# Twenty-one streams of unread matmuls, with other orders of the moving columns, between the memory stage and layer 0 of an encoder

## The chip, the core and the metric

The kernel runs on one core of a Trainium2 chip. The core has five engines that run side by side and meet through semaphores: TensorE (matmuls, PE in the profile, its weight loads PEld), VectorE (DVE), ScalarE (ACT), GpSimd (POOL) and SyncE (SP, which here issues the transfers). SBUF is the on-chip memory of 128 partitions that the engines read, PSUM the one that matmuls write. The metric is the time of one execution on the device in microseconds (us).

## The reference

A trunk of two layers over 256 tokens of width 2048 in float32. Each layer projects the normed tokens with one wide matrix, runs a short gated convolution, a differential attention and a cross-attention into 256 memory tokens on parts of the result, and projects back:

```python
for l in range(DEPTH):
    h = rmsnorm(x, norm_g[l])
    proj = h @ w_in[l]
    ...
    mn = rmsnorm(mem, mem_norm_g[l])
    mkv = mn @ w_mem_kv[l]
    ...
    y = jnp.concatenate([y_a, y_d, y_m], axis=-1) @ w_out[l]
    x = x + y
```

w_in[l] is 2048 x 7168, w_mem_kv[l] 2048 x 1024 and w_out[l] 2048 x 2048, so nearly all the work is in these products.

## The kernel before

Every large product is done in three matmuls of type float32r: each operand is split into a rounded part (hi) and the rest (lo), and the products hi*hi, hi*lo and lo*hi are summed in PSUM (L227, L228, L229). The stationary side is the transposed activation: memT for the memory, xT for a layer's input, yT for its mixed output. Each of these is one tile of 128 partitions x 2 parts x 16 slices x 256 tokens: part 0 is hi, part 1 is lo, and slice k holds the features 128k to 128k+127. So the hi part of a partition is one row of 4096 neighbouring float32r numbers, and slice k is its columns 256k to 256k+255. The moving side is the weight: block() (L218) computes 512 output columns for both halves of the tokens (NT = 2), and for each of the 16 slices of the weight there are 2 x 3 matmuls, so 96 in a block. A weight slice comes by DMA into raw (four buffers of two slices, issued by SyncE), ScalarE casts it to hi (L210, or L213 with a gain) and VectorE subtracts to get lo (L211, L214). hi and lo have eight buffers each, so eight slices can be in store ahead of TensorE.

The memory stage comes first: for each layer two blocks with memT (keys and values). During its later blocks, small pieces of other work run between the matmuls from a list called side. One of them, x_rows, transposes x on TensorE into the PSUM tile pt (L468), and split_T writes it into xT (ScalarE L192, VectorE L193). Behind the memory stage flush_side() ends the list, and the layers begin. Block 0 of layer 0 gives the first 512 columns of the attention's queries and keys; normed() computes their squares (ScalarE, L275), a sum and an inverse root in small steps on VectorE (L276 to L282) and the scaled result nat (L284). During block 1, qk_T transposes nat on TensorE into ptq (L356) and copies it into yT (ScalarE L364, VectorE L365).

The order in which each engine runs is not the order of the code. The program is built with a scheduler that simulates the engines and gives each of them its own list, in which independent pieces of code are interleaved. PSUM tiles come from pools: acc from ps_acc (four buffers), and the attention scores s from ps_s (two buffers). A tile that takes a buffer waits on a semaphore until the last users of that buffer are done.

Of the kernel before, what the change touches and what calls it, by code (L numbers as in the profile page):

```python
# [10 lines left out]
F32 = mybir.dt.float32  # L11
# [7 lines left out]
P = 128  # L19
# [13 lines left out]
NB = 512  # L33
# [10 lines left out]
def encoder(ctx: ExitStack, tc: tile.TileContext, x, mem, norm_g, w_in, conv_w, conv_b,  # L44
            dq_g, dk_g, lq1, lk1, lq2, lk2, head_g, mem_norm_g, w_mem_kv, mq_g, mk_g, w_out, out):
    nc = tc.nc
    x, mem, out = x[0], mem[0], out[0]

    def pool(name, bufs, space=None):
        kw = {"space": space} if space is not None else {}  # L50
        return ctx.enter_context(tc.tile_pool(name=name, bufs=bufs, **kw))
# [8 lines left out]
    ps_s = pool("ps_s", 2, PSUM)  # L60
# [121 lines left out]
    def flush_side():  # L182
        while side:
            run_side()
# [292 lines left out]
    def stats_of(parts, tag):  # L477
        ss = small.tile([P, NT], F32, tag="ssum", name=nm("ssum"))
        nc.vector.tensor_reduce(ss, parts, AX.X, ALU.add)
        return row_stats(ss, tag)  # L480

    def T_tile(what):
        return big.tile([P, 2, KT, SEQ], F32R, tag="T", name=nm(what))
# [38 lines left out]
    for l in range(DEPTH):  # L522
# [13 lines left out]
        if l == 0:  # L536
            side.append(turn(nat, [(mkT[l], 0, MH, cvb[:, 56 + l:57 + l])]))
            xT = T_tile("xT")
# [3 lines left out]
                    x_square(c, t)  # L542
    flush_side()

    for l in range(DEPTH):
        st = stats_of(ssx, "st")

# [105 lines left out]
        if l + 1 < DEPTH:  # L653
            xT = T_tile("xT")
        order = list(range(CG, KT)) + list(range(CG))
        for b in range(4):
            final = l + 1 == DEPTH
            acc = block(yT, w_out[l], [(b * NB, NB)], order, apart=4 if final and b == 3 else 0)
            for t in range(NT):
                n = 256 if final else NB  # L660
# [41 lines left out]
```

## Time and profile before

| | us |
|---|---|
| median of 2 runs (964.81 to 964.99) | 964.9 |
| the profiled execution's own time | 965.74 |
| its span, first to last instruction | 964.0 |

The profile is of one execution. In its groups of instructions a row has the line, the engine, the operation, output and inputs by their names in the program, the shapes and the count; then the busy time in all in us, the mean of one in ns, and the idle time of the engine in front of them. In its timeline a row has the start in us from the beginning of the span, the duration in us, engine, line and operation. In a table by stretches each row has the stretch, its length, then busy time and count of instructions of TensorE, its weight loads, VectorE, ScalarE and GpSimd, the clock granted to TensorE (1.00 is full), the share of the DMA engines that is busy and GB/s. The end of a matmul is modelled, since matmuls overlap: starts are what the pace is read from. The weight loads of float32r matmuls stand in the profile as rows of their own, and in the lists of instructions below they belong to the matmul.

### The profile page before, as it was taken

What the parts mean: (1) busy time and instruction counts of PE and PEld (TensorE: products, weight loads), DVE (VectorE), ACT (ScalarE), POOL (GpSimd) and SP (SyncE); (2) the same over time, 40 slices, a digit from 0 to 9 for tenths busy, and PEclk for the clock granted to TensorE, in tenths of its full rate; (3) what the DMA queues carried; (4) which work ended last, traced back from release to release, by engine and by line L of the source; (5) the groups of instructions that cost most, each with busy time, mean ns of one, the idle gap of its engine ahead of it and who ended that gap; (6) DMA issues with size and microseconds to landing.
All of it is one profiled execution on the core that took longest, in us unless ns stands there. A gap on an engine that the chain in (4) does not pass through costs nothing.

```text
span 964.0 us, 13420 instructions
## 1 busy us (share of the span) xinstructions
PE 956.4 (99%) x4485; PEld 791.5 (82%) x4485; DVE 671.1 (70%) x1496; ACT 561.1 (58%) x1103; POOL 1.4 (0%) x8
## 2 busy tenths in 40 slices
PE   9999999999999999999999999999999999999998
PEld 6788888888888888888888888888888888888886
DVE  5768568865787876567766678866787776578553
ACT  7676555765656655554555556754666655554442
POOL 0000000000000000000000000000000000000000
PEclk9999999999999999999999999999999999999999
DMA  8855666566555555555555666666555565555662
GB/s 293 281 182 182 185 189 187 175 198 195 175 169 160 156 172 162 168 174 175 189 182 178 194 176 181 180 207 197 153 172 177 155 176 154 175 174 175 217 217 68
DMA packets 101353, 175.26 MB, mean 182 GB/s; under 512 B 6190, under 2 KB 25764, under 8 KB 101284
## 3 DMA queue, kind: packets, MB, share of 16 engines
q1 hardware_dynamic: 100132, 173.36, 59.3%
q10 hardware_dynamic: 1152, 1.05, 0.3%
q8 instruction: 35, 0.57, 0.2%
q14 instruction: 34, 0.28, 0.1%
HBM read 172.29 MB, written 2.10 MB: 181 GB/s over the span
## 4 chain that ended last, share of the span: by engine, by line
PE 96%; ACT 1%; DMA 1%; DVE 0%; SPq 0%; issue 0%; DVEq 0%; ACTq 0%
PE acc L229 30%; PE acc L227 30%; PE acc L228 30%; PE po L330 2%; DMA raw<-in_w_mem_kv_dram 1%; PE ptT L323 1%; PE pt L468 1%; PE s L438 1%; PE s L392 1%; PE s L391 1%; ACT hi L213 1%; PE ptq L356 1%; ACT sq L519 1%; PE py L315 0%; PE pt L296 0%; PE pt L602 0%
## 5 line engine op out<-in xcount | busy, mean ns | idle before, releaser
L210 ACT CAST hi<-raw 128x512 fp32r<-128x512 f32 x576 | 356.3, 622 | 324.9 <-PE acc L229 200.0
L211 DVE TENSOR_TENSOR lo<-raw,hi 128x512 fp32r<-128x512 f32 x576 | 395.7, 690 | 209.8 <-ACT hi L210 204.9
L227 PE MATMUL acc<-hi,xT 128*128 128x512 f32 x896 | 354.0, 395 | 0.0
L228 PE MATMUL acc<-lo,xT 128*128 128x512 f32 x896 | 352.0, 393 | 0.0
L229 PE MATMUL acc<-hi,xT 128*128 128x512 f32 x896 | 351.7, 392 | 0.0
L227 PEld LDWEIGHTS acc<-hi,xT 128*128 128x128 f32 x896 | 168.4, 188 | 33.8
L229 PEld LDWEIGHTS acc<-hi,xT 128*128 128x128 f32 x896 | 168.4, 188 | 33.8
L228 PEld LDWEIGHTS acc<-lo,xT 128*128 128x128 f32 x896 | 168.5, 188 | 33.3
L228 PE MATMUL acc<-lo,yT 128*128 128x512 f32 x256 | 99.9, 391 | 0.0
L229 PE MATMUL acc<-hi,yT 128*128 128x512 f32 x256 | 99.2, 390 | 0.0
L227 PE MATMUL acc<-hi,yT 128*128 128x512 f32 x256 | 98.3, 392 | 0.0
L214 DVE SCALAR_TENSOR_TENSOR lo<-raw,cva,hi 128x512 fp32r<-128x512 f32 x64 | 47.3, 749 | 19.2 <-ACT hi L213 18.2
L213 ACT ACTIVATE hi<-raw,cva 128x512 fp32r<-128x512 f32 x64 | 44.9, 721 | 24.1 <-PE acc L229 12.1
L229 PEld LDWEIGHTS acc<-hi,yT 128*128 128x128 f32 x256 | 48.1, 188 | 10.0
L228 PEld LDWEIGHTS acc<-lo,yT 128*128 128x128 f32 x256 | 48.1, 188 | 9.7
L227 PEld LDWEIGHTS acc<-hi,yT 128*128 128x128 f32 x256 | 48.1, 188 | 9.7
L227 PE MATMUL acc<-hi,memT 128*128 128x512 f32 x128 | 51.9, 409 | 1.4 <-ACT memT L189 0.9
L228 PE MATMUL acc<-lo,memT 128*128 128x512 f32 x128 | 50.3, 394 | 0.0
L229 PE MATMUL acc<-hi,memT 128*128 128x512 f32 x128 | 48.5, 396 | 0.0
L227 PEld LDWEIGHTS acc<-hi,memT 128*128 128x128 f32 x128 | 24.3, 190 | 7.2 <-ACT memT L189 1.6
L228 PEld LDWEIGHTS acc<-lo,memT 128*128 128x128 f32 x128 | 24.4, 190 | 4.7
L229 PEld LDWEIGHTS acc<-hi,memT 128*128 128x128 f32 x128 | 23.9, 188 | 5.1 <-DVE memT L190 0.2
(150 smaller groups left out, 685.0 us busy)
## 6 DMA issues: line engine op xcount, KB each, us to landing
raw<-in_w_in_dram SPq DMA_DIRECT2D x192, 512.0 KB, 3.9
raw<-in_w_out_dram SPq DMA_DIRECT2D x64, 512.0 KB, 3.7
raw<-in_w_in_dram SPq DMA_DIRECT2D x64, 256.0 KB, 3.5
raw<-in_w_mem_kv_dram SPq DMA_DIRECT2D x31, 512.0 KB, 4.7
xs<-in_x_dram SPq DMA_DIRECT2D x4, 512.0 KB
xs<-in_mem_dram SPq DMA_DIRECT2D x3, 512.0 KB, 9.7
out_dram<-xs SPq DMA_DIRECT2D x8, 128.0 KB, 3.3
out_dram<-xs ACTq DMA_DIRECT2D x8, 128.0 KB
```

Source lines behind the costliest of these rows:

```text
L210: nc.scalar.copy(hi, raw[:, j])
L211: nc.vector.tensor_tensor(lo_, raw[:, j], hi.bitcast(F32), ALU.subtract)
L213: nc.scalar.activation(hi, raw[:, j], AF.Copy, scale=gains_of(j))
L214: nc.vector.scalar_tensor_tensor(lo_, raw[:, j], gains_of(j), hi.bitcast(F32), ALU.mult, ALU.subtract)
L227: nc.tensor.matmul(acc[t], sh, hi, start=first, stop=False)
L228: nc.tensor.matmul(acc[t], sh, lo, start=False, stop=False)
L229: nc.tensor.matmul(acc[t], sl, hi, start=False, stop=last)
L323: nc.tensor.transpose(pt[:, k, i * P:(i + 1) * P], e[:, i, k * P:(k + 1) * P], ident)
L330: nc.tensor.matmul(po[:, i, :], eT[:, k, i * P:(i + 1) * P], v[:, k, h * P:(h + 1) * P], start=k == 0, stop=k == NT - 1)
L356: nc.tensor.transpose(pt[:, j, :], nat[t][:, j * P:(j + 1) * P], ident)
L391: nc.tensor.matmul(s[c][:, i, :], qi, k_first(yT, c, h), start=True, stop=False)
L392: nc.tensor.matmul(s[c][:, i, :], qi, k_second(yT, k2, c, h), start=False, stop=True)
```

## The change

One function and 21 calls are added behind the flush_side() of the memory stage. Nothing else is touched.

```diff
@@ -542,6 +542,41 @@
                     x_square(c, t)
     flush_side()
 
+
+    flat = xT[:, 0].rearrange("p k t -> p (k t)")
+
+    def stream(name, base=512, run=None, jump=None, turned=False, n=6):
+        ps = ps_s.tile([P, NB], F32, tag="s", name=name)
+        o, mov = ps, flat[:, base:base + NB]
+        if run is not None:
+            mov = mov.rearrange("p (l q i) -> p q l i", i=run, q=jump // run)
+            if turned:
+                o = o.rearrange("p (l q i) -> p q l i", i=run, q=jump // run)
+        for j in range(n):
+            nc.tensor.matmul(o, flat[:, 0:P], mov, start=True, stop=True)
+
+    stream("prA")
+    stream("prB", run=2, jump=4)
+    stream("prC", run=2, jump=8)
+    stream("prD", run=2, jump=16)
+    stream("prE", run=2, jump=32)
+    stream("prF", run=2, jump=64)
+    stream("prG", run=2, jump=128)
+    stream("prH", run=2, jump=256)
+    stream("prI", run=4, jump=16)
+    stream("prJ", run=4, jump=64)
+    stream("prK", run=8, jump=16)
+    stream("prL", run=8, jump=64)
+    stream("prM", run=16, jump=32)
+    stream("prN", run=16, jump=256)
+    stream("prO", base=514)
+    stream("prP", base=516)
+    stream("prQ", base=520)
+    stream("prR", base=528)
+    stream("prS", run=2, jump=16, turned=True)
+    stream("prT", run=2, jump=64, turned=True)
+    stream("prU", base=514, run=2, jump=16)
+
     for l in range(DEPTH):
```

Each stream is six equal matmuls: the first 128 columns of xT's hi part are the stationary tile, 512 columns from base are the moving ones, and the product goes into a PSUM tile of the scores' pool, which nothing reads. With run and jump the same 512 columns are taken in another order: run neighbours, then the run that lies jump columns further on, and so on to the end of the 512, and then the same from the next run. prA to prR and prU write their output in the order in which the columns come. prS and prT are turned: they write each column to its own place, so the output jumps as the input does.

The scheduler does not put all of them in front of layer 0. TensorE's list at the end of the memory stage, before (xT_669 is xT; acc_1197 and acc_1198 are the two halves of block 0, with one number for each tile):

```order
L468 MATMUL pt_1093<-ident,xs 128x128 [waits DVE_49,PE_49]
L468 MATMUL pt_1093<-ident,xs 128x128 x3
L227 MATMUL acc_1197<-hi_1201,xT_669 128x512
L228 MATMUL acc_1197<-lo_1202,xT_669 128x512
L229 MATMUL acc_1197<-hi_1201,xT_669 128x512
```

And with the change, where acc_1344 and acc_1345 are the two halves of block 0:

```order
L468 MATMUL pt_1093<-ident,xs 128x128 [waits DVE_49,PE_49]
L468 MATMUL pt_1093<-ident,xs 128x128 x3
L556 MATMUL prA<-xT_669 128x512 x6
L556 MATMUL prB<-xT_669 128x512 x6
L227 MATMUL acc_1344<-hi_1348,xT_669 128x512
...
L227 MATMUL acc_1344<-hi_1370,xT_669 128x512
L556 MATMUL prC<-xT_669 128x512 [waits PE_49]
L556 MATMUL prC<-xT_669 128x512 x5
L556 MATMUL prD<-xT_669 128x512 [waits PE_49]
L556 MATMUL prD<-xT_669 128x512 x5
L228 MATMUL acc_1344<-lo_1371,xT_669 128x512
```

Two streams stand in front of block 0. The others follow two at a time, with 13 matmuls of the blocks between pairs: prC to prP in block 0, prQ to prT in block 1, and prU by itself behind them. From prC on the first matmul of each stream waits on TensorE's own semaphore, for the last users of its PSUM buffer.

The second place is in block 1, where TensorE transposes the queries and keys of block 0 (ptq_1427 and ptq_1458; acc_1403 and acc_1404 are the halves of block 1). Before:

```order
L227 MATMUL acc_1404<-hi_1517,xT_669 128x512
L228 MATMUL acc_1404<-lo_1518,xT_669 128x512
L356 MATMUL ptq_1427<-ident,nat_1398 128x128 [waits DVE_49,PE_49]
L356 MATMUL ptq_1427<-ident,nat_1398 128x128 x3
L356 MATMUL ptq_1458<-ident,nat_1401 128x128 [waits DVE_49,PE_49]
L356 MATMUL ptq_1458<-ident,nat_1401 128x128 x3
L229 MATMUL acc_1404<-hi_1517,xT_669 128x512
```

With the change (ptq_1574 and ptq_1605; acc_1550 and acc_1551 are the halves of block 1):

```order
L556 MATMUL prS<-xT_669 128x8x32x2 [waits PE_49]
L556 MATMUL prS<-xT_669 128x8x32x2 x5
L556 MATMUL prT<-xT_669 128x32x8x2 [waits PE_49]
L556 MATMUL prT<-xT_669 128x32x8x2 x5
L227 MATMUL acc_1551<-hi_1589,xT_669 128x512
...
L227 MATMUL acc_1550<-hi_1616,xT_669 128x512
L356 MATMUL ptq_1574<-ident,nat_1545 128x128 [waits DVE_49]
L356 MATMUL ptq_1574<-ident,nat_1545 128x128 x3
L356 MATMUL ptq_1605<-ident,nat_1548 128x128 [waits DVE_49]
L356 MATMUL ptq_1605<-ident,nat_1548 128x128 x3
L228 MATMUL acc_1550<-lo_1617,xT_669 128x512
L556 MATMUL prU<-xT_669 128x512 [waits PE_49]
```

In block 1 the transposes stood behind 59 of its matmuls. Now they stand behind 25 of them and the 24 of prQ to prT.

The third place is VectorE's list in block 1, the small steps between the squares of block 0 and nat. Before (lo_1518, lo_1536 are casts of block 1's slices 10 and 11):

```order
L159 TENSOR_SCALAR rsy_1384<-rsy_1384 128x16 [waits DVE_49]
L161 SCALAR_TENSOR_TENSOR rsa_1385<-rsy_1384 128x16 [waits DVE_49]
L211 TENSOR_TENSOR lo_1518<-raw_1511,hi_1517 128x512 [waits Activation_49]
L162 TENSOR_TENSOR rsa_1385<-rsa_1385,ss_1375 128x16 [waits DVE_49]
L163 SCALAR_TENSOR_TENSOR rsy_1384<-rsa_1385,rsy_1384 128x16 [waits DVE_49]
L161 SCALAR_TENSOR_TENSOR rsa_1385<-rsy_1384 128x16 [waits DVE_49]
L211 TENSOR_TENSOR lo_1536<-raw_1533,hi_1535 128x512 [waits DMAHW6_49,Activation_49]
```

With the change (lo_1665 is the cast of slice 10):

```order
L159 TENSOR_SCALAR rsy_1531<-rsy_1531 128x16 [waits DVE_49]
L161 SCALAR_TENSOR_TENSOR rsa_1532<-rsy_1531 128x16 [waits DVE_49]
L162 TENSOR_TENSOR rsa_1532<-rsa_1532,ss_1522 128x16 [waits DVE_49]
L163 SCALAR_TENSOR_TENSOR rsy_1531<-rsa_1532,rsy_1531 128x16 [waits DVE_49]
...
L284 TENSOR_TENSOR nat_1545<-acc_1344,rsy_1531 128x512 [waits DVE_49]
L284 TENSOR_TENSOR nat_1548<-acc_1345,rsy_1531 128x512 [waits DVE_49]
L211 TENSOR_TENSOR lo_1665<-raw_1658,hi_1664 128x512 [waits Activation_49]
```

The casts of slices 10 to 13 stood between the small steps. Three of them now stand behind nat, and the one of slice 13 behind the four copies of ptq into yT (L365). ScalarE's list changes in the same place and in the same way: its four copies of ptq (L364) now stand together, and so do its last two into xT (L192), with VectorE's last two (L193). The lists of SyncE and GpSimd are as before.

## The prediction

> **What bounds the kernel now.** I read the page first, then the waits of TensorE, then the stretches, and last the timeline at single instructions. The page's first rows and the chain of work that ended last:
>
> ```profile
> span 964.0 us, 13420 instructions
> PE 956.4 (99%) x4485; PEld 791.5 (82%) x4485; DVE 671.1 (70%) x1496; ACT 561.1 (58%) x1103; POOL 1.4 (0%) x8
> PEclk9999999999999999999999999999999999999999
> PE 96%; ACT 1%; DMA 1%; DVE 0%; SPq 0%; issue 0%; DVEq 0%; ACTq 0%
> ...
> L227 PE MATMUL acc<-hi,xT 128*128 128x512 f32 x896 | 354.0, 395 | 0.0
> L227 PEld LDWEIGHTS acc<-hi,xT 128*128 128x128 f32 x896 | 168.4, 188 | 33.8
> ```
>
> TensorE is busy for 956.4 of 964.0 us at full granted clock, and 96% of the chain is matmuls. A busy TensorE is not yet a TensorE at its pace, so the next question is whether it waits near the change. All waits of TensorE (time in total, times, longest), and stretches from the start, around the change and at the end:
>
> ```profile
> PE warm L112 <- DVE zeros L107: 1.2, 1, 1.2
> PE pt L468 <- DMA xs<-in_mem_dram: 1.1, 2, 0.9
> PE acc L227 <- ACT memT L189: 0.9, 1, 0.9
> PE acc L227 <- ACT hi L213: 0.5, 1, 0.5
> ...
> 0.00:20.00 20.00, 17.68 (x71) 11.76 (x72) 10.94 (x25) 16.08 (x37) 1.37 (x8) 1.00 0.84 291
> 20.00:50.00 30.00, 28.57 (x130) 22.62 (x129) 23.36 (x66) 18.45 (x33) 0.00 (x0) 1.00 0.83 282
> ...
> 100.00:120.00 20.00, 20.00 (x96) 16.55 (x94) 10.91 (x18) 12.55 (x22) 0.00 (x0) 1.00 0.60 171
> 120.00:150.00 30.00, 30.00 (x138) 24.94 (x137) 22.05 (x45) 16.37 (x28) 0.00 (x0) 1.00 0.62 186
> ...
> 900.00:964.00 64.00, 60.16 (x266) 49.48 (x264) 31.35 (x54) 23.03 (x37) 0.00 (x0) 0.99 0.51 165
> ```
>
> The second column is TensorE's busy time in each stretch. It stands idle for 2.3 us before 20 us, 1.4 us before 50 us, and 3.8 us at the end where only output is left. In the two stretches around the change it has no idle time at all. So there is no hole there which added matmuls could fill, and every matmul put in front of layer 0 pushes the end out by its own pace.
>
> **The pace of one matmul** is not its duration (395 ns in the group of the page), since the next one starts before the last one has drained. It is the distance between starts. Timeline of TensorE, start, duration, engine, line (PEld is the weight load):
>
> ```profile
> 94.31 0.39 PE L229 MATMUL acc<-hi,memT 128*128 128x512 f32 x1
> 94.31 0.19 PEld L227 LDWEIGHTS acc<-hi,memT 128*128 128x128 f32 x1
> 94.54 0.39 PE L227 MATMUL acc<-hi,memT 128*128 128x512 f32 x1
> 94.54 0.19 PEld L228 LDWEIGHTS acc<-lo,memT 128*128 128x128 f32 x1
> 94.76 0.39 PE L228 MATMUL acc<-lo,memT 128*128 128x512 f32 x1
> ...
> 196.35 0.39 PE L227 MATMUL acc<-hi,xT 128*128 128x512 f32 x1
> 203.83 0.39 PE L227 MATMUL acc<-hi,xT 128*128 128x512 f32 x1
> ```
>
> The last two rows are 33 matmuls apart: 7.48 / 33 = 0.2267 us each. The weight load of the next one (0.19 us) runs under it. In that stretch every sixth matmul waits on a semaphore of ScalarE and a weight tile changes each time, and both are inside the 0.2267.
>
> **The change, part by part.** It removes nothing. It adds 21 streams of 6 matmuls, 126 in all, each with a 128x128 stationary tile from xT, 512 moving columns from xT and a PSUM tile that nobody reads. They have the form of the rows above. No engine but TensorE gets an instruction, and no DMA is added.
>
> 1. 126 x 0.2267 = 28.6 us, if every order of columns streams at the pace of a contiguous one. The bound from below is the weight load, which each matmul has: 126 x 0.188 (mean of the LDWEIGHTS group above) = 23.7 us. No row of before reads its moving columns in another order than one run after the other, so the trace has no price for this. The bound from above is the slowest row per column, the plain fp32 scores of the memory heads:
>
> ```profile
> L438 PE MATMUL s<-mkT,mqT 128*128 128x256 f32 x32 | 8.2, 378 | 0.0
> ...
> 403.12 1.03 PE L438 MATMUL s<-mkT,mqT 128*128 128x256 f32 x4
> 403.80 0.58 PE L227 MATMUL acc<-hi,xT 128*128 128x512 f32 x1
> 404.22 0.39 PE L228 MATMUL acc<-lo,xT 128*128 128x512 f32 x1
> ```
>
> From 403.12 to 404.22 are four of them and one L227: (1.10 - 0.2267) / 4 = 0.218 us for 256 columns, so 0.437 us for 512. An order that halves the rate costs 0.437 - 0.227 = 0.21 us more per matmul, and if all 126 ran so the streams would take 55.1 us. I take the contiguous pace for all: five streams (A, O, P, Q, R) are contiguous in all but their start, and the other sixteen still read whole runs of 2 to 16 neighbours, so they are nearer to the rows at 0.2267 than to a form that runs at half rate because of its type. [...]
>
> 2. The seams. The streams stand in ten pairs and one single between the matmuls of blocks 0 and 1, so there are 22 seams. What a seam can cost is seen where TensorE changes its kind of work:
>
> ```profile
> 107.49 0.60 PE L468 MATMUL pt<-ident,xs 128*128 128x128 f32 x4
> 107.84 0.48 PE L227 MATMUL acc<-hi,xT 128*128 128x512 f32 x1
> 108.16 0.40 PE L228 MATMUL acc<-lo,xT 128*128 128x512 f32 x1
> ```
>
> The first L227 after transposes takes 0.32 us to the next start, 0.09 more than usual: at most 22 x 0.09 = 2.0 us. I take 0, because the streams have the type and shape of their neighbours and a change of tile alone costs nothing in the rows at 196 us. Nineteen streams (all but prA and prB) also wait for TensorE's own earlier matmuls, the last users of their PSUM buffer. Those are at least 11 matmuls back, so 11 x 0.2267 = 2.5 us, long past the 0.39 us that one takes. Queued behind such a wait is only TensorE's own order. 0.
>
> 3. The moved work. The eight transposes into ptq stood 59 matmuls behind the start of block 1 and now stand 49 behind it, 24 of them streams, so at 11.1 us instead of 13.4. They wait for VectorE's nat. VectorE now runs that chain of small steps with fewer casts (lo) between. Its rows in before, where block 1 starts at 129.74:
>
> ```profile
> 129.74 0.39 PE L227 MATMUL acc<-hi,xT 128*128 128x512 f32 x1
> 129.89 1.36 DVE L276 TENSOR_REDUCE ss<-sq 128x8 f32<-128x512 f32 x2
> 132.64 0.17 DVE L158 TENSOR_SCALAR rsy<-ss 128x16 int32<-128x16 int32 x1
> 132.84 0.17 DVE L159 TENSOR_SCALAR rsy<-rsy 128x16 int32<-128x16 int32 x1
> 137.05 0.36 DVE L282 TENSOR_SCALAR rsy<-rsy,st 128x8 f32<-128x8 f32 x2
> 138.00 1.28 DVE L284 TENSOR_TENSOR nat<-acc,rsy 128x512 f32<-128x512 f32 x2
> ```
>
> Up to L158 the order is as before (2.9 us behind the start of the block). Then 11 small steps of 0.2 us, 0.36 and 1.28 follow without casts: nat is there 6.8 us behind the start, 4.3 us ahead of the transposes that wait for it. The casts that VectorE puts off are those of the slices 10 to 13 of block 1. TensorE wants slice 10 behind 54 block and 30 stream matmuls and the transposes, 19.9 us in, and VectorE has it by 6.8 + 0.69 = 7.5 us. The four yT steps then hold VectorE until about 15 us, and slice 13 is wanted at 24.0. So nothing waits: 0. The cover is the eight slices of hi and lo in store, about 48 x 0.2267 = 10.9 us; were it gone, a late nat would hold TensorE for what it is late, and no more than these few us once.
>
> 4. SyncE's weight DMAs are neither moved nor added to. They come later with the buffers they wait for. ScalarE and VectorE get 28.6 us more for the same work. Since TensorE does not wait for them after 50 us, that wins nothing.
>
> Sum against the profiled execution: 964.0 + 28.6 = 992.6 us of span, 965.74 + 28.6 = 994.3 us for its own time. The median of the runs is 0.84 us under the profiled one: 964.9 + 28.6 = **993.5 us**. The likeliest case's own range is 992.0 to 995.5, the upper end with the 2.0 us of seams.
>
> **The rivals.**
>
> - Turned output. prS and prT also write PSUM in the pairs' order. If that alone runs at half rate, 12 x 0.21 = 2.5 us more: 996.0 us, and 1001 at a third or so of the rate. No row of before writes a matmul's output in short runs, and all of its outputs are contiguous, which speaks neither way. [...] Chance 0.12.
> - Pairs read at half rate. Eight streams read runs of 2 without turning (B to H and U), two with. 60 x 0.21 = 12.6 us more: 1006.1 us. For it: the contiguous pace needs a column every 0.44 ns, and half rate is what the plain fp32 rows show this engine falling to. Against it: the pair is still a run. Chance 0.14.
> - Every broken order is slow, runs of 4 to 16 too: 96 x 0.21 = 20.2 us more, 1013.7 us, or beyond if the rate falls further for far jumps. Chance 0.06.
> - The other side: not slower by 2%. One mechanism could do it: six matmuls in a row keep the same stationary tile, and if TensorE then ran at the pace of its short matmuls, there would be little to pay. It decides below 19.3 / 126 = 0.153 us each. The nearest row, ptq's eight transposes in 0.87 us on the chain, has 0.109 each, which gives 13.7 us and 978.6 us.
>
> ```profile
> 143.28 0.87 PE ptq L356 x8
> ```
>
> Against it stand the rows at 94.54 and 94.76: L228 has the same stationary tile as L227 ahead of it, yet loads it again and starts 0.22 us later. [...] Chance 0.02.
>
> The remaining 0.06 goes to mixtures between 995.5 and 1006: one far jump that is slow, or an odd start that costs.
>
> **How the numbers follow.** The likeliest is 993.5 us, with 0.60. The range goes from 991.0, a little under the likeliest case, to 1007.0, which takes in the turned output and the slow pairs: 0.60 + 0.12 + 0.14 and most of the mixtures, and leaves out the slow case for all orders and the other side. A change of 2% (19.3 us) is about what a measurement of this kernel tells from none, so the line for slower is 984.2 us. All cases but the other side lie above it: slower 0.97, within 2% 0.02, and faster 0.01, since nothing is removed.
>
> **What would show it.** In the changed kernel the starts within each stream should lie 0.227 us apart for all 21 names, with prS and prT the likeliest to differ, then prB to prH. TensorE's busy time should be some 985 us with the same four waits, no wait of ptq for nat, and the granted clock at 1.00 in the stretch of the streams. The prediction is wrong if a stream's starts lie 0.4 us apart or 0.15, if TensorE shows idle time between 105 and 180 us, or if the time added is not 126 times the pace.

## The result and the profile after

The changed kernel takes 1007.97 us (median of 2 runs, 1007.92 to 1008.02) against 964.9 us: 43.1 us more, ratio 1.0446 with a 95% interval from 1.0401 to 1.0491. The forecast was 993.5 us in a range of 991.0 to 1007.0, so the direction was right, the size was not, and the time lies 1.0 us outside the range.

The page of the changed kernel, span and busy time:

```profile
span 1006.2 us, 13671 instructions
PE 998.8 (99%) x4611; PEld 816.6 (81%) x4611; DVE 671.2 (67%) x1496; ACT 561.5 (56%) x1103; POOL 1.4 (0%) x8
```

TensorE has 126 matmuls more (4611 against 4485) and is busy for 42.4 us longer, where 28.6 us were forecast. The other engines do what they did before. All of its waits, and the two stretches with the streams (columns as in the table of stretches before):

```profile
PE acc L227 <- ACT memT L189: 1.3, 1, 1.3
PE warm L112 <- DVE zeros L107: 1.2, 1, 1.2
PE pt L468 <- DMA xs<-in_mem_dram: 1.2, 2, 0.7
```

```profile
100.00:150.00 50.00, 50.00 (x183) 34.24 (x183) 13.53 (x21) 14.18 (x25) 0.00 (x0) 1.00 0.32 95
150.00:185.00 35.00, 35.00 (x141) 25.70 (x140) 15.94 (x37) 11.39 (x19) 0.00 (x0) 1.00 0.28 83
```

No new wait has come, and one of the four of before is gone. The moved transposes ptq wait for nothing (nat is written by 167.8 us, they start at 175.1), the granted clock is at 1.00, and TensorE has no idle time from 100 to 185 us. In 50 us it ran 183 matmuls and transposes there, where a pace of 0.2267 us gives some 220. So the time went into the matmuls themselves. The timeline of TensorE, the streams and the rows that follow them:

```profile
107.50 1.64 PE L556 MATMUL prA<-xT 128*128 128x512 f32 x6
108.98 2.87 PE L556 MATMUL prB<-xT 128*128 128x512 f32 x6
111.66 0.42 PE L227 MATMUL acc<-hi,xT 128*128 128x512 f32 x1
...
125.72 3.20 PE L556 MATMUL prF<-xT 128*128 128x512 f32 x6
128.74 0.41 PE L229 MATMUL acc<-hi,xT 128*128 128x512 f32 x1
...
134.40 2.15 PE L556 MATMUL prH<-xT 128*128 128x512 f32 x6
136.38 0.40 PE L227 MATMUL acc<-hi,xT 128*128 128x512 f32 x1
...
164.25 1.53 PE L556 MATMUL prR<-xT 128*128 128x512 f32 x6
165.62 0.39 PE L229 MATMUL acc<-hi,xT 128*128 128x512 f32 x1
...
168.59 2.75 PE L556 MATMUL prS<-xT 128*128 128x512 f32 x6
171.17 3.15 PE L556 MATMUL prT<-xT 128*128 128x512 f32 x6
174.14 0.41 PE L227 MATMUL acc<-hi,xT 128*128 128x512 f32 x1
```

From the start of a stream to the next row's start, divided by six, is its pace: (165.62 - 164.25) / 6 = 0.228 us for prR, (111.66 - 108.98) / 6 = 0.447 for prB. All 21, worked out so:

| streams | order of the columns | us for each matmul |
|---|---|---|
| prA, prO to prR | contiguous, from 512, 514, 516, 520 and 528 | 0.247 (prA, behind transposes), 0.228 to 0.235 |
| prI, prK to prN | runs of 4, 8, 16 | 0.228 to 0.243 |
| prJ | runs of 4, jump 64 | 0.277 |
| prB to prE, prG, prU | runs of 2 | 0.428 to 0.458 |
| prS | runs of 2, jump 16, turned | 0.430 |
| prF, prT | runs of 2, jump 64; prT turned | 0.503, 0.495 |
| prH | runs of 2, jump 256 | 0.330 |

Together they take 42.4 us, and the span is 42.2 us longer. The ten streams that read pairs take 26.6 us of it instead of the 13.6 that a contiguous pace gives.

### The profile page after: what moved, and what is told of

Read it like the earlier page. It is cut to its first block, busy times and chain, and to the rows that moved or that the text cites. A ratio compares the mean times of both kernels' runs of the same rounds, so it can differ in the third digit from the quotient of the medians.

```text
span 1006.2 us, 13671 instructions
## 1 busy us (share of the span) xinstructions
PE 998.8 (99%) x4611; PEld 816.6 (81%) x4611; DVE 671.2 (67%) x1496; ACT 561.5 (56%) x1103; POOL 1.4 (0%) x8
## 4 chain that ended last, share of the span: by engine, by line
PE 97%; DMA 1%; ACT 1%; SPq 0%; DVE 0%; issue 0%; DVEq 0%; ACTq 0%
PE acc L227 29%; PE acc L229 28%; PE acc L228 28%; PE po L330 2%; PE ptT L323 1%; DMA raw<-in_w_mem_kv_dram 1%; PE pt L468 1%; DMA xs<-in_mem_dram 1%; PE s L438 1%; PE s L392 1%; PE s L391 1%; PE ptq L356 1%; PE py L315 0%; ACT hi L213 0%; ACT sq L519 0%; PE pt L296 0%
## 5 line engine op out<-in xcount | busy, mean ns | idle before, releaser
L213 ACT ACTIVATE hi<-raw,cva 128x512 fp32r<-128x512 f32 x64 | 45.1, 721 | 23.3 <-PE acc L229 13.6
```

What stands on the lines that cost most here:

```text
L213: nc.scalar.activation(hi, raw[:, j], AF.Copy, scale=gains_of(j))
```

## The experiments

In all of them the streams stand at the same place, six matmuls each, and nothing else of the program is changed. Paces are worked out as above. The kernels that put other streams in place of the 21 were run once each, so their paces come from one trace; orders that stand in several kernels repeat within 6%.

**Are the streams all of it?** One kernel keeps the eleven streams that read no pairs, one the other ten.

```diff
-    stream("prB", run=2, jump=4)
...
-    stream("prH", run=2, jump=256)
...
-    stream("prS", run=2, jump=16, turned=True)
-    stream("prT", run=2, jump=64, turned=True)
-    stream("prU", base=514, run=2, jump=16)
```

> Leaves out the ten streams that read runs of 2 (prB to prH, prS, prT, prU) and keeps the other eleven. In the trace of the changed kernel those eleven take 15.7 us together, 0.237 us a matmul. Theory that the time is nothing but the pace of each stream: 964.9 + 15.7 = 980.6 us. Rival, that the schedule or the waits of the whole change cost something by themselves: more than 983.

> Keeps only the ten streams that read runs of 2. In the trace of the changed kernel they take 26.8 us together, 0.447 us a matmul. Theory of the pace alone: 964.9 + 26.8 = 991.7 us, and the gain over no streams adds up with the kernel that has the other eleven to the 43.1 us of the whole change. Rival, that the streams are slow because of something that runs beside them at their place (casts, transfers): pace of single streams changes with the place, and the sum is off by more than 2 us.

The first took 981.58 us against 965.3 (16.3 more, ratio 1.0169, interval 1.0152 to 1.0186; 980.6 expected), the second 991.71 (26.4 more, 1.0281, 1.0265 to 1.0296; 991.7 expected). The sum is 42.7 us and the whole change 43.1. Each stream kept its pace within 6% though it stood up to 33 us earlier and had other neighbours. So the cost is the pace of each stream, and the pairs' half is what was missing in the forecast.

**Lines or breaks?** The first theory was that each visit to a line (the name here for four columns from a multiple of four on) has a price, the rival that each break in the order has one.

```diff
+    put("qd", part(512, 4, 16))
+    put("qe", part(514, 4, 16))
...
+    put("qk", again(4))
+    put("ql", plain, lambda t: turn_(t, 2, 16))
...
+    put("qn", part(512, 1, 16))
```

part(base, run, jump) is the order of the change's streams, again(n) reads each pair n times in a row, and the third argument of put turns the output alone.

> Other streams in the place of the 21, six matmuls each. Theory LINE: the moving side is read in lines of 4 float32r columns, and each visit to a line costs about 1.75 ns (0.447 us / 256 pairs), whether 2 or 4 columns are taken from it. Theory RUN: each break in the sequence costs that, wherever it lies. Both: run 2 jump 16 (qc) 0.447, run 4 on line starts (qd) 0.23, runs of 8 and 16 on line starts (qf, qh) 0.23, single columns with jump 16 (qn) 0.89, pairs in one pass with steps 4, 6, 8, 16 (qo to qr) 0.447, runs of 4 with step 8 (qs) 0.23. They differ at: run 4 from column 514 (qe) LINE 0.447, RUN 0.23; run 8 from 514 (qg) LINE 0.336, RUN 0.23; run 16 from 514 (qi) LINE 0.28, RUN 0.23; each pair read twice or four times in a row (qj, qk) LINE 0.23, RUN 0.447; every second column (qu) LINE 0.447, RUN 0.89. Turned output alone, with contiguous input (ql, qm): 0.23 if PSUM does not mind pairs, 0.44 if it does.

Timeline of TensorE in this kernel:

```profile
115.60 1.52 PE L551 MATMUL qd<-xT 128*128 128x512 f32 x6
116.96 0.39 PE L228 MATMUL acc<-lo,xT 128*128 128x512 f32 x1
...
119.91 2.85 PE L551 MATMUL qe<-xT 128*128 128x512 f32 x6
122.58 1.58 PE L551 MATMUL qf<-xT 128*128 128x512 f32 x6
...
139.35 1.46 PE L551 MATMUL qk<-xT 128*128 128x512 f32 x6
140.65 1.54 PE L551 MATMUL ql<-xT 128*128 128x512 f32 x6
142.03 0.39 PE L229 MATMUL acc<-hi,xT 128*128 128x512 f32 x1
...
144.97 1.52 PE L551 MATMUL qm<-xT 128*128 128x512 f32 x6
146.33 2.76 PE L551 MATMUL qn<-xT 128*128 128x512 f32 x6
148.91 0.41 PE L227 MATMUL acc<-hi,xT 128*128 128x512 f32 x1
```

Runs of 4 take 0.227 us on line starts (qd) and 0.445 from column 514 (qe), where each run lies half in one line and half in the next. Runs of 8 and 16 from 514 took 0.333 and 0.283. Pairs read four times in a row (qk) take 0.217. All of this goes against the price of a break and fits lines. The turned output (ql, qm) takes 0.230 and 0.227, beside 0.230 for a contiguous order (qb): output in pairs cost nothing here. Every second column (qu, two from each line in a visit) takes 0.450, as LINE said. But single columns (qn), with twice as many visits, take 0.430 and not 0.89. So the visits do not have one price, and LINE fell as it stood.

**Is a line held?** prH's 0.330 us raised the question whether a line that is visited again soon is cheaper.

```diff
+    put("wc", lanes(256))
+    put("wd", lanes(260))
...
+    put("wm", lanes(128, 4))
+    put("wq", lanes(68, 8))
```

lanes(d, n) takes pairs in turn from n stretches that lie d columns apart.

> Other streams in the place of the 21: pairs taken in turn from n lanes that lie d columns apart, so that a line is visited again after n-1 other lines. prH (two lanes, 256 apart) took 0.330 us instead of 0.447, prF and prT (eight lanes, 64 apart) 0.50. Theory HELD: two lines can be held at once, so every kernel of two lanes (wc to wl, d from 256 to 2048) runs at 0.23 to 0.33 whatever d is, and four or eight lanes at 0.447. Theory BANK: the distance decides; two lanes at 256, 512, 1024, 2048 differ from 260 to 288, and eight lanes at 68 (wq) run at 0.447 where 64 (wo, wp) runs at 0.50. wb repeats prH (0.33), wo prF (0.50), ws prJ (0.277); wt (run 4, jump 256) and wu (run 4, jump 32) 0.23.

Two lanes took 0.327 to 0.340 us at all ten distances from 256 to 2048, four lanes 0.447 and 0.443. So the distance does not decide it: prH and all ten streams of two lanes come back to a line after one other, and take 0.33 us or so instead of prB's 0.447. Coming back after three others (four lanes) gained nothing. Eight lanes took 0.49 to 0.50 at distances of 64 and 512 and 0.460 at 68, so there the distance does matter, by 6 to 8%.

**What inside a line counts?**

```diff
+    put("hg", part(512, 1, 256))
+    put("hn", step(8, 4, 1))
+    put("hs", plain.rearrange("p (l q i) -> p l i q", q=2, i=2))
+    put("ht", plain.rearrange("p (l q i) -> p l i q", q=2, i=4))
```

step(s, run, base) takes run columns of every s.

> Single columns with jump 16 took 0.430 us, not the 0.89 of LINE, so a visit to a line does not have one price. Two theories are left. VISIT: a visit that takes one column costs 0.87 ns, one that takes 2, 3 or 4 costs 1.75 ns. COLUMN: a column costs 0.44 ns only where all four of a line follow one another, and 0.87 ns anywhere else. Both: single columns with jumps 4, 8, 64, 128 (hc to hf) 0.43 to 0.45; pairs in the middle of a line (hj) and across two lines (hk) 0.447; runs of 4 that lie 2 and 2 in two lines (ho) 0.447; runs of 6 as 4 and 2 (hp) 0.30; runs of 6 as 1, 4, 1 (hq) 0.30; runs of 10 as 4, 4, 2 (hr) 0.27. They differ at runs of 4 that lie 3 and 1 (hn): VISIT 0.335, COLUMN 0.447. Order inside a line, columns 0 2 1 3 (hs) and pairs swapped, 2 3 0 1 (hv): 0.23 if only the line counts, 0.447 if neighbours must follow one another upwards. Two lines in turn, 0 4 1 5 2 6 3 7 (ht) and single columns from two lanes (hg): 0.43, or between 0.23 and 0.34 if a line is held over one other. Runs of 4 from two lanes (hu) 0.23 to 0.25.

Timeline of TensorE: hg, hn and ht, each with the row behind it:

```profile
129.21 1.46 PE L554 MATMUL hg<-xT 128*128 128x512 f32 x6
130.51 2.93 PE L554 MATMUL hj<-xT 128*128 128x512 f32 x6
...
139.00 2.90 PE L554 MATMUL hn<-xT 128*128 128x512 f32 x6
141.69 0.44 PE L228 MATMUL acc<-lo,xT 128*128 128x512 f32 x1
...
160.04 1.46 PE L554 MATMUL ht<-xT 128*128 128x512 f32 x6
161.34 0.39 PE L228 MATMUL acc<-lo,xT 128*128 128x512 f32 x1
```

Both theories missed. Single columns from two lanes (hg) took 0.217 us, a full pace with no two neighbours in a row; from four lanes (hf) 0.283; two lines in turn (ht) 0.217; columns 0 2 1 3 (hs) 0.225; pairs swapped (hv) 0.232. Runs of 4 that lie 3 and 1 (hn) took 0.448, the runs of 6 and 10 (hp, hq, hr) 0.303, 0.303 and 0.280.

One estimate fits all of these. It is worked out from the paces alone: the columns at the even places of the order and those at the odd places are added up apart, as two sides, and the dearer side is the pace. A column counts about 0.87 ns (0.217 to 0.23 us / 256), and a line that the side has not just had counts 1.75 ns (0.447 us / 256), whether one or two columns are taken from it in that visit. The expectations below call it TWO READERS, with a reader for a side and a held line for one that it has just had; no trace shows such readers. The estimate leaves out he, single columns from eight lanes 64 apart: these took 0.498 us, as slow as pairs from eight lanes at that distance. In a contiguous order each side finds two columns in each line, so the lines add nothing. In the order 0 1, then elsewhere, each finds one, at 1.75 ns: 256 x 1.75 = 0.448 us, where prB took 0.447. With single columns each side has 256 lines too: 0.448 again, where jumps of 4, 8 and 16 (hc, hd, qn) took 0.457, 0.432 and 0.430. In hn one side has both of its columns in one line and the other has them in two lines, and the dearer side gives the 0.448.

**Is it bytes or columns?**

```diff
+    half = flat.bitcast(mybir.dt.bfloat16)
+    full = flat.bitcast(F32)
...
+    put("yc", of(half, 1024, 1, 32), sta=half[:, 0:P])
+    put("yh", full[:, 512:1024], sta=full[:, 0:P])
+    put("ys", lanes(64, 16))
```

> The same bits of xT read as bf16 (yb to yg), as plain fp32 (yh to yk), and eight or more lanes of pairs in float32r (ym to yu). BYTES theory: what must follow one another is 16 bytes, so in bf16 runs of 8 (yf) stay at 0.22 to 0.23, runs of 4 (ye), of 2 (yd), single ones (yc) and runs of 8 that lie 4 and 4 in two lines (yg) take 0.43 to 0.447. COLUMNS theory: four columns in a row are enough whatever their width, so ye and yg stay at 0.23 too. Plain fp32, contiguous (yh): 0.437 as in the kernel before; if it reads its columns twice at the float32r pace, runs of 4 (yi) 0.44 and pairs and single ones (yj, yk) 0.87 to 0.9; if it is slow inside the array, all four 0.44. Lanes: BANK, distances that are multiples of 64 columns (ym 64, yr 128, ys 64 with 16 lanes, yt 64 with 64 lanes) take 0.50 and 66, 72, 80, 96 (yn to yq) 0.447; if the number of eight lanes does it, ym to yr all take about the same and ys, yt, yu 0.447.

The tiles of four of these streams: shortest, median and longest duration in ns, then first and last start in us:

```profile
L554 PE MATMUL yc<-xT x6: 1017/1033/1034, 112.9 to 117.1; 128*128 128x512 bf16 x6
L554 PE MATMUL yd<-xT x6: 607/607/609, 118.0 to 120.1; 128*128 128x512 bf16 x6
L554 PE MATMUL ye<-xT x6: 376/377/390, 123.5 to 124.6; 128*128 128x512 bf16 x6
L554 PE MATMUL yh<-xT x12: 591/592/592, 130.5 to 135.2; 128*128 128x512 f32 x12
```

Five distances lie between six starts. In bf16 single columns take (117.1 - 112.9) / 5 = 0.84 us, pairs 0.42 and runs of 4 0.22, as contiguous ones do: single columns and pairs come to 1.64 ns for each run (0.84 / 512 and 0.42 / 256), with no sides to add up apart. BYTES fell: runs of 4, half as many bytes as in float32r, stay at 0.22, as COLUMNS said. The last row shows what was not known before: a plain fp32 matmul stands in the profile as two rows. Six of them have twelve, 4.7 / 11 = 0.43 us apart, so one costs 0.86 us. In fp32 pairs cost no more (0.86), and single columns twice as much (1.71). Sixteen and 64 lanes of float32r pairs at distance 64 took 0.540 and 0.560. Eight lanes at 72, 80 and 96 took 0.443 to 0.458, at 128 0.487 and at 66 0.485. BANK had set 66 at 0.447, so a distance that is a multiple of 64 is not the whole of it.

**Does the run's length alone undo it?** The ten streams read runs of 4 instead.

```diff
-    stream("prD", run=2, jump=16)
+    stream("prD", run=4, jump=16)
...
-    stream("prT", run=2, jump=64, turned=True)
+    stream("prT", run=4, jump=64, turned=True)
```

> All 21 streams stay, the ten that read pairs read runs of 4 on line starts (prB and prC both with jump 8, prU from column 512). Theory that the size of the run is the whole cause: 126 matmuls at 0.23 to 0.28 us (0.277 with jump 64: prF, prJ, prT) are 31 us, so 965.3 + 31 = 996 us, 12 us under the whole change. Rival, that jumps or turned output cost by themselves: over 1000.

It took 995.94 us against 965.03, ratio 1.0320 (1.0303 to 1.0338): 12 us under the whole change, where 996 was expected. The jumps and both turned outputs were in place (only prB's jump grew, from 4 to 8, and prU started at 512 instead of 514).

**The estimate put to the test.** By it pairs need not cost anything if each side finds its two columns in one line. The ten streams read pairs again, the first two columns of each group of s = 4, 8, 12 or 16, and take them from two groups in turn: 0 s 1 s+1.

```diff
+    def in_turn(name, s, base=0, n=6):
+        ps = ps_s.tile([P, NB], F32, tag="s", name=name)
+        mov = flat[:, base:base + s * NB // 2].rearrange("p (x l s) -> p x l s", l=2, s=s)[:, :, :, 0:2]
+        for j in range(n):
+            nc.tensor.matmul(ps, flat[:, 0:P], mov.rearrange("p x l i -> p x i l"), start=True, stop=True)
...
-    stream("prB", run=2, jump=4)
-    stream("prC", run=2, jump=8)
-    stream("prD", run=2, jump=16)
+    in_turn("prB", 4)
+    in_turn("prC", 8)
+    in_turn("prD", 16)
```

> All 21 streams and 126 matmuls stay. The ten that read pairs now read, in one pass, the first two columns of every group of 4, 8, 12 or 16, and take them from two groups in turn: 0 s 1 s+1, then the next two groups. The same pairs in order 0 1 s s+1 took 0.44 to 0.46 us (run of 2 with steps 4, 8, 16). Theory TWO READERS: float32r columns are read by two readers, one for the even and one for the odd places of the order, and each needs about 1.75 ns for a line it does not hold and 0.87 ns for each column. Here each reader finds its two columns in one line, so the ten run at 0.23 us: 15.9 + 60 x 0.23 = 29.7 us, 965.0 + 29.7 = 994.7 us. Rival LINE or COLUMN (a line of which only two columns are taken, or two that do not follow each other, costs double): the ten stay at 0.44, 1007 us or more.

Timeline of TensorE:

```profile
109.61 1.54 PE L562 MATMUL prB<-xT 128*128 128x512 f32 x6
110.99 0.40 PE L227 MATMUL acc<-hi,xT 128*128 128x512 f32 x1
...
113.98 1.47 PE L562 MATMUL prC<-xT 128*128 128x512 f32 x6
115.29 1.47 PE L562 MATMUL prD<-xT 128*128 128x512 f32 x6
116.60 0.39 PE L228 MATMUL acc<-lo,xT 128*128 128x512 f32 x1
...
164.75 2.08 PE L562 MATMUL prU<-xT 128*128 128x512 f32 x6
166.66 0.41 PE L229 MATMUL acc<-hi,xT 128*128 128x512 f32 x1
```

995.58 us against 964.82 (1.0314, 1.0297 to 1.0331), 994.7 expected. prB, prC and prD take 0.230, 0.218 and 0.218 us. They take the same pairs as qo, qq and qr in the experiment on lines, which read them in the order 0 1 s s+1 and took 0.452, 0.458 and 0.442. The order of the same pairs alone makes the factor of two. One stream did not fit: prU, groups of 12, with 0.318.

**Orders made for the estimate.** Another kernel has streams that the estimate sets apart from a theory of runs, and some in bf16.

```diff
+    put("ic", single(1024, 2, 2))
+    put("id", single(1024, 2, 4))
+    put("ie", in_turn(0, True))
+    put("if", in_turn(0, False))
+    put("ig", single(260, 4))
+    put("ih", single(512, 6))
+    put("ii", single(512, 8))
...
+    put("io", half[:, 1024:1536].rearrange("p (l q) -> p q l", l=2), sta=sh)
```

single(d, n, s) takes every s-th column, one at a time, in turn from n stretches d columns apart; in_turn reads pairs of groups of 8 in turn (True) or in order (False).

> Theory TWO READERS in float32r (1.75 ns for a line not held, 0.87 ns a column, each reader holds two lines): single columns from two lanes, every second column (ic) 0.23, every fourth (id) 0.45; pairs of two groups of 8 in turn (ie) 0.23, the same pairs in order (if) 0.45; single columns from four lanes (ig), where each reader has two lines in turn, (2 x 1.75 + 6 x 0.87) / 8 x 256 = 0.28; from six lanes (ih), three lines in turn for each reader, 0.44 if only two lines are held and 0.28 if more are; from eight lanes (ii) 0.44 to 0.50. ONE READER in bf16 (1.67 ns for a line, 0.42 ns a column): contiguous (ik, ip) 0.22, single columns with jump 32 (il) 0.85, pairs (im) 0.43, runs of 4 (in) 0.22, single columns from two lanes (io) 0.29 if two lines are held and 0.85 if not. Under a theory of runs or of neighbours ic, ie and io would be at twice the contiguous pace or more.

```profile
113.54 1.52 PE L554 MATMUL ic<-xT 128*128 128x512 f32 x6
114.90 2.88 PE L554 MATMUL id<-xT 128*128 128x512 f32 x6
117.60 0.41 PE L228 MATMUL acc<-lo,xT 128*128 128x512 f32 x1
...
120.61 1.47 PE L554 MATMUL ie<-xT 128*128 128x512 f32 x6
121.92 2.94 PE L554 MATMUL if<-xT 128*128 128x512 f32 x6
124.67 0.41 PE L229 MATMUL acc<-hi,xT 128*128 128x512 f32 x1
```

In this timeline of that kernel ic takes 0.227 us, id 0.450, ie 0.218 and if 0.458, all four as written down ahead. Four lanes of single columns (ig) took 0.272 (0.28 expected). Six lanes took 0.295, so in the estimate three lines in turn on a side still count as just had; eight lanes took 0.498. In bf16 two lanes of single columns (io) took 0.485, between the two numbers expected, and no run shows why.

**The stream that did not fit.**

```diff
+    put("jb", turns(3, 6))
+    put("jg", turns(1, 6))
+    put("jt", step(24, 4))
```

turns(d, s) reads pairs in turn from two lines that lie d lines apart, with s lines from step to step; step(4s, 4) reads a run of 4 in every s-th line.

> With the pairs in turn nine of ten streams ran at 0.217 to 0.230 us, but prU (groups of 12 columns) at 0.318. Here are the same pairs in turn with the two readers d lines of 4 columns apart and s lines from one step to the next: (3,6) again (jb, now at another place), (1,2) to (1,8) (jc to ji), (2,4) to (2,8) (jj to jn), (3,7), (3,8), (4,8) (jo to jq), and runs of 4 with steps of 3, 5, 6, 7 lines (jr to ju). TWO READERS alone: all 0.22 to 0.23. PLACE theory (prU was slow because it stood beside the ptq transposes): jb 0.22 like the rest. DISTANCE theory (the lines' addresses matter too): jb 0.32 again, and others with it, so that which d and s are slow shows what the distance has to be; runs of 4, where both readers are in one line, 0.23 at each step.

Timeline of TensorE: jb with s = 6, jc and jd with 2 and 3, then runs of 4 with s = 5 and 6 (js, jt):

```profile
109.58 2.08 PE L554 MATMUL jb<-xT 128*128 128x512 f32 x6
111.49 0.41 PE L227 MATMUL acc<-hi,xT 128*128 128x512 f32 x1
...
114.46 1.54 PE L554 MATMUL jc<-xT 128*128 128x512 f32 x6
115.84 1.50 PE L554 MATMUL jd<-xT 128*128 128x512 f32 x6
...
161.41 1.76 PE L554 MATMUL js<-xT 128*128 128x512 f32 x6
163.00 2.08 PE L554 MATMUL jt<-xT 128*128 128x512 f32 x6
164.92 0.40 PE L227 MATMUL acc<-hi,xT 128*128 128x512 f32 x1
```

PLACE fell: jb, far from the transposes ptq, has 0.318 us as prU had. In these streams the pace goes by s alone: 0.265 for 5 lines (20 columns) and 0.318 to 0.320 for 6 lines (24 columns), with d from 1 to 3 and for whole lines too, and 0.217 to 0.235 for 2, 3, 4, 7 and 8. The estimate puts all of them at 0.22 to 0.23, so it lacks what the step from line to line does. Why 5 and 6 are slow stays open, and so does why eight or more lanes are slow at distances of 64, 66, 128 and 512 columns and not at 68 to 96: these runs show where, not what it is.

## Why the prediction was wrong, point by point

- **What bounds the kernel** was right: no idle time to fill, no new wait, and 126 matmuls in front of the rest push the end by their own pace (42.4 us of streams, 42.2 us of span).
- **Term 1, the price of an order, failed.** It took the contiguous pace for all 126, on the ground that a run of two neighbours is nearer to a contiguous order than to a form that is slow because of its type. The contiguous pace was right for 66 of them (15.8 us against 15.0). The 60 that read pairs cost 26.6 us instead of 13.6. What the runs showed in its place: a matmul that reads pairs in order takes 0.43 to 0.46 us, and with the same pairs taken from two lines in turn 0.218 to 0.230. By the estimate from those runs, what matters is how many columns the even and the odd places of the order each find in a line, and in a pair that is one. The rival "pairs read at half rate" had this, with 0.21 us more a matmul (measured 0.22) and 1006.1 us, at a chance of 0.14. The range followed that rival's number but left it under 1 us above. Little things carried the time past its end: 0.8 us of the streams without pairs; 0.4 us of the pairs, where prF and prT at jump 64 are slower than the rest and prH is faster; and 0.7 us between the difference of the medians (43.1) and the streams (42.4). That last part is within the 1.8 us over which the kernel before spread in later runs (964.5 to 966.3).
- **The bound from above was misread.** The rows of L438 were taken for one matmul each, but a plain fp32 matmul has two rows: the program has 16 matmuls on L438 (four heads, two halves, two layers), the page 32 rows. One of 512 columns costs 0.86 us, so these rows' real bound was twice the 0.437 that the text used. That the pairs came out at 0.447 was luck and not the reason given.
- **Term 2, the seams**, 0 taken and at most 2.0 us: right. prA behind transposes has 0.12 us more in all, and the eleven streams without pairs exceed the pace by 0.8 us together, of which prJ alone has 0.3.
- **Terms 3 and 4, moved work and transfers**: right. ptq did not wait for nat, and VectorE, ScalarE and SyncE stayed off the path.
- **Turned output** was wrong as a rival: with the output alone turned, in pairs, ql and qm took 0.230 and 0.227 us. Output in runs of one was not tried. One of the rival's two times was also added up wrongly: at a third of the rate 12 matmuls cost 5.4 us more, which gives 998.9 us, and 1001 needs about a quarter.
- **The other side** was wrong: the six equal stationary tiles were loaded six times. PEld has 126 loads more, and no float32r stream went under 0.215 us.

## What to carry to other kernels

When a float32r matmul reads its moving columns out of order, count for the even and for the odd places separately how many columns each finds in a line (four columns from a multiple of four on) before it moves on. For 512 columns here two meant 0.217 to 0.230 us in most orders, and one meant 0.43 to 0.50 where the order did not soon come back to the line. Whole aligned lines in another order cost nothing or little (0.227 us at jump 16, 0.277 at jump 64), pairs in order 0.22 us more a matmul, and pairs taken from two lines in turn nothing (0.218 to 0.230); steps of 5 or 6 lines (0.265 and 0.32) are to be avoided. A price that the trace does not show should keep its whole bound in the range, and before a row is taken as a bound its count must be held against the program: here one matmul had two rows.

## What the runs showed of the hardware that was not expected

- Neighbours were not needed in float32r: 512 single columns from two stretches 256 apart (hg) took 0.217 us.
- Coming back to a line soon was cheaper than going to another each time: single columns from six lanes took 0.295 us, and with jumps of 4 to 16 columns 0.430 to 0.457. In the six lanes each side comes back to a line after two others.
- A start off the line costs a contiguous order next to nothing (0.235 us from 514, 0.228 to 0.235 from the line starts 516, 520 and 528), but runs of 4 from 514 took 0.445 us against 0.227 from 512.
- Steps of 20 and 24 columns from line to line took 0.265 and 0.32 us, with 12, 16, 28 and 32 columns at 0.217 to 0.235.
